# First loads in eight pieces from two queues, a fixed order of the first roundings, eight warm-up products, and pe copied mostly by ScalarE

## The chip, the cores and the metric

The kernel runs on one core of one Trainium2 chip. A core has TensorE (PE, matrix products into PSUM), VectorE (DVE), ScalarE (ACT), GpSimd (POOL) and SyncE (SP, here the engine that issues DMAs). The metric is device microseconds of one execution, lower is better. The kernel before takes 1084.98 us, the median of 3 runs (1084.43 to 1085.68).

## The reference

One layer of a decoder trunk, all in float32, for 1024 tokens of width 1024:

```
h = rms_norm(x, norm_mix_g)
proj = h @ w_in          # q, k, v, z_a, gate, conv B, C, xc, z_c, merge gates g_a, g_c
y_a = (rms_norm(gated linear attention(q, k, v, gate)) * silu(z_a)) @ w_branch_a
y_c = (B * causal_dwconv3(C * xc) * silu(z_c)) @ w_branch_c
x = x + (sigmoid(g_a + b_ga) * y_a + sigmoid(g_c + b_gc) * y_c) @ w_out
gate = sigmoid(rms_norm(x, norm_ple_g) @ w_ple_gate)
x = x + gate * (p @ w_ple_proj)
out = rms_norm(x, norm_final_g)
```

What matters here is `p @ w_ple_proj`, called pe: p is 1024 x 256, the weight 256 x 1024. It depends on nothing but inputs. It is the first real work of the kernel; its result is stored to DRAM and read again near the end.

## The kernel before

Every large product is done in three passes over fp32r operands: each operand is split into a rounded high part and a low part (`hi`, and `lo = src - hi`), and high x high, high x low and low x high are added up in PSUM (`mm3`, line 605). `split` (594) is one rounding copy on ScalarE and one subtraction on VectorE. The large projections use a scheme of seven products of half-size quadrants instead of eight; each quadrant product is a chain of 128x128 by 128x512 products in one PSUM bank.

The program is first written down as a list of operations (`Flow.note`, 270), and a planner puts them in order: `set_dues` (369) counts a due time back from the end, `put_in_order` (416) replays all engines with estimated costs and picks, whenever an engine is free, the ready operation with the earliest due time. TensorE's main products stay in the order in which they were written; products marked as side work (`nc.side`), such as the sums `ms` and the transposes `rt`, are slipped in when ready. `nc.hurry` moves due times earlier. All DMAs are issued by SP, in the order of the plan.

The start runs like this. VectorE clears `zero` (929), and TensorE does nine products of zeros into the banks that pe will use (934), the warm-up. Meanwhile SP loads the first halves of p transposed (`pr_`, in the trace `pTraw`) and of the pe weight (`wr_`, in the trace `wperaw`), each in two pieces of 128 x 512 (kt = 0 and 1), 256 KB a piece (956 to 958). Then come the second half of the weight, x transposed (`hq`) and the rest of p. The pieces are split (1041 to 1045) into `pThi`, `pTlo`, `wpehi`, `wpelo`.

`pe_blocks` (1007) multiplies: a block is 128 tokens by 512 columns, six products (two kt, three passes) in one of six banks. The first four blocks go through kt first: for kt 0 each block's three passes, then the same for kt 1. Each finished block is copied out of PSUM, by VectorE for odd blocks and by ScalarE for even ones (1021), and stored to DRAM (`ped`). There are 16 blocks.

Beside that, `scale_h` (976) computes the norm of x: squares on ScalarE (`sq`), their sums over the partitions on TensorE (`ms`), the power -0.5 on GpSimd (`r_x`), a copy on VectorE that spreads the four columns of `r_x` over 128 columns each (`rb`, 994), four transposes on TensorE (`rt`), and the scaling of `hq` on VectorE. Then `h0hi` and `h0lo` are split off, and the first cells, `ga0p` to `ga3p`, are multiplied with them (`two_products`, 1030). `Cell.product` (751) goes through four kt, three passes each.

The lines that set the first products' order are these:

```
todo = [(b, kt) for kt in range(2) for b in bs] if by_kt else [(b, kt) for b in bs for kt in range(2)]
for b, kt in todo:
    mm3(acc[b - bs[0]], pth[:, kt, rows(b)], ptl[:, kt, rows(b)], wph[:, kt, halves[c]],
        wpl[:, kt, halves[c]], kt == 0, kt == 1)
```

Of the kernel before, what the change touches and what calls it, by code (L numbers as in the profile page):

```python
# [9 lines left out]
F32 = mybir.dt.float32  # L10
# [6 lines left out]
P = 128  # L17
# [239 lines left out]
class Flow:  # L257
# [4 lines left out]

    def __init__(self, tc):
        nc = tc.nc
        self.tc, self.ops, self.side, self.open, self.hurry, self.bundle = tc, [], True, [], 0.0, None
        self.tensor, self.vector, self.scalar = Port(self, PE, nc.tensor), Port(self, DVE, nc.vector), Port(self, ACT, nc.scalar)
        self.gpsimd, self.sync = Port(self, POOL, nc.gpsimd), Port(self, SP, nc.sync)


    def note(self, engine, op, call, args, kw):  # L270
        views = [a for a in args if isinstance(a, View) or hasattr(a, "ap")]
        views += [a for k, a in kw.items() if k not in ("out", "accum_out") and (isinstance(a, View) or hasattr(a, "ap"))]
        outs, ins = ([kw["out"]], views) if "out" in kw else (views[:1], views[1:])
        if kw.get("accum_out") is not None:
            outs.append(kw["accum_out"])
        o = Op()
        o.n, o.engine, o.call, o.args, o.kw = len(self.ops), engine, call, args, kw
        o.side, o.table, o.bytes, o.bufs, o.hurry = self.side, 0, 0, [], self.hurry
        label = lambda v: v.buf.name if isinstance(v, View) else "in"
        o.name = f"{label(outs[0])}<-{','.join(label(v) for v in ins)}"  # L280
        shape = outs[0].shape
        n = 1
        for d in shape[1:]:
            n *= d
        o.lat = 0.15
        if engine == PE:
            o.cost, o.lat = n / 2400 + 0.0134, 0.22
            if op == "transpose" or args[1].dtype == F32:
                o.cost = 0.11
            elif args[1].shape[0] < P:  # L290
                o.cost = 0.42
        elif engine == DVE:
            psum = any(isinstance(v, View) and v.buf.pool.name == "ps" for v in outs + ins)
            o.cost = 0.07 + n * (0.00055 if op in ("tensor_scalar", "tensor_copy") and not psum else 0.00104)
            if op in ("scalar_tensor_tensor", "tensor_scalar"):
                o.cost += 0.06
            if op == "tensor_tensor_scan":
                o.cost = 0.05 + n * 0.0021
        elif engine == ACT:
            o.cost = 0.10 + n * 0.000833 + (0.1 if "accum_out" in kw else 0.0)  # L300
            o.table = TABLE.get(args[2] if len(args) > 2 else None, 0)
        elif engine == POOL:
            o.cost = 0.1 + n * 0.001 if op == "memset" else 0.6
        else:
            o.cost, o.bytes = 0.4, shape[0] * n * 4
            if getattr(ins[0], "apart", None):
                o.cost, o.bytes = 0.6, 1.4 * o.bytes
            o.lat = 2.0 + o.bytes / 250e3
        preds = {}

        def behind(p):
            if p is not None and p != o.n:
                q = self.ops[p]
                lat = q.lat
                if q.engine == engine and engine != SP:
                    lat = 0.0 if engine == PE else 0.08
                preds[p] = max(preds.get(p, 0.0), lat)

        for v in ins:
            if isinstance(v, View):  # L320
                for b in v.blocks():
                    e = v.buf.memory.setdefault(b, [None, []])
                    behind(e[0])
                    e[1].append(o.n)
        for v in outs:
            if isinstance(v, View):
                for b in v.blocks():
                    e = v.buf.memory.setdefault(b, [None, []])
                    for p in [e[0]] + e[1]:
                        behind(p)  # L330
                    e[0], e[1] = o.n, []
                if engine == PE:
                    behind(v.buf.group)
                    v.buf.group = o.n
                for pool in v.buf.pool.instead:
                    for old in pool.buffers:
                        for p in old.users:
                            behind(p)
        for v in outs + ins:
            if isinstance(v, View) and v.buf not in o.bufs:  # L340
                if v.buf.index is None:
                    v.buf.index = len(v.buf.tag.buffers)
                    v.buf.tag.buffers.append(v.buf)
                o.bufs.append(v.buf)
                v.buf.users.append(o.n)
        o.preds, o.succs = preds, []
        for p in preds:
            self.ops[p].succs.append(o.n)
        self.ops.append(o)
        if self.bundle is not None and engine == PE:  # L350
            self.bundle.append(o)
# [163 lines left out]
def kernel(  # L515
# [22 lines left out]
    def f(ap):  # L538
        return ap.bitcast(F32)
# [186 lines left out]
    class Cell:  # L726
# [21 lines left out]
                self.load(k)  # L748
                self.ring[k] = self.steps[k]()

        def product(self, k, acc, start):
            self.prep(k)
            shi, slo = self.ring[k]
            rhi, rlo = self.res[k]
            for kt in range(4):
                nc.side = False
                mm3(acc, shi[:, kt, :], slo[:, kt, :], rhi[:, kt, :], rlo[:, kt, :], start and kt == 0, kt == 3)
                nc.side = True
                if kt % 2 == 1:
                    tick()  # L760
# [165 lines left out]

    hres = [None] * 7
    zero = bp.tile([P, 512], F32R, tag="u2", name="zero", bufs=2)
    nc.vector.memset(f(zero), 0.0)
    ones = sm.tile([P, 1], F32, name="ones")  # L930
    nc.gpsimd.memset(ones, 1.0)
    warm = [psm.tile([P, 512], F32, tag=f"m{i}", name=f"warm{i}") for i in range(6)]
    nc.side = False
    for n in range(9):
        mm(warm[n % 6], zero[:, 0:P], zero, start=True, stop=True)
    nc.side = True

    with phase("prep0") as pool:
# [15 lines left out]

        nc.hurry = 8.0
        for kt in range(2):
            load(pr_[:, kt, halves[0]], pT[:, kt, halves[0]])
            load(wr_[:, kt, halves[0]], wpe[:, kt, halves[0]])
        for kt in range(2):
            load(wr_[:, kt, halves[1]], wpe[:, kt, halves[1]])  # L960
        nc.hurry = 0.0
# [14 lines left out]
        def scale_h(i):  # L976
# [13 lines left out]
            r = sm.tile([P, 4], F32, tag="rx", name=f"r_x{i}", bufs=2)  # L990
            nc.vector.tensor_scalar(r, sums[:, :, 0], EPS, None, op0=ALU.add)
            nc.gpsimd.tensor_tensor(r, r, mhalf[:, 0:1].to_broadcast([P, 4]), op=ALU.pow)
            rb = bp.tile([P, 4, P], F32, tag="u2", name=f"rb{i}", bufs=2)
            nc.vector.tensor_copy(rb, r[:, :, None].to_broadcast([P, 4, P]))
            rt = pso.tile([P, 4, P], F32, tag="o", name=f"rt{i}", bufs=2)
            for s in range(4):
                transpose(rt[:, s, :], rb[:, s, :])
            rt = rt.rearrange("p s t -> p (s t)")
            for n in both:
                for k in range(4):  # L1000
# [6 lines left out]
        def pe_blocks(bs, c, by_kt=False):  # L1007
            acc = []
            for b in bs:
                n = BANKS[at[0]] if at[0] < len(BANKS) else 4 + at[0] % 2  # L1010
                acc.append(psm.tile([P, 512], F32, tag=f"m{n}", name=f"pe{b}_{c}"))
                at[0] += 1
            todo = [(b, kt) for kt in range(2) for b in bs] if by_kt else [(b, kt) for b in bs for kt in range(2)]
            for b, kt in todo:
                nc.side = at[0] > len(BANKS)
                mm3(acc[b - bs[0]], pth[:, kt, rows(b)], ptl[:, kt, rows(b)], wph[:, kt, halves[c]],
                    wpl[:, kt, halves[c]], kt == 0, kt == 1)
                nc.side = True
                if kt == 1:
                    t = bp.tile([P, 512], F32, tag="T", name=f"pe{b}_{c}", bufs=4)  # L1020
                    (nc.vector.tensor_copy if b % 2 else nc.scalar.copy)(t, acc[b - bs[0]])
                    store(ped[b][:, halves[c]], t)

        hb, steps = build_a("h", q)
# [5 lines left out]
        def two_products(cells, banks):  # L1030
            acc = [psm.tile([P, 512], F32, tag=f"m{n}", name=f"{c.name}X") for n, c in zip(banks, cells)]
            for c, X in zip(cells, acc):
                c.product(0, X, True)
                t = ev(f"{c.name}s1")
                nc.scalar.copy(t, X)
                store(s1d[pre.index(c)], t)
            for c, X in zip(cells, acc):
                c.product(3, X, False)
                c.cons(0, 0, X)

        nc.hurry = 8.0
        for kt in range(2):
            split(pth[:, kt, halves[0]], ptl[:, kt, halves[0]], pr_[:, kt, halves[0]])
            split(wph[:, kt, halves[0]], wpl[:, kt, halves[0]], wr_[:, kt, halves[0]])
        nc.hurry = 0.0
        pe_blocks(range(0, 4), 0, True)
        split_half(wph, wpl, wr_, 1)
# [754 lines left out]
```

## Time and profile before

| what | us |
|---|---|
| median of 3 runs | 1084.98 |
| profiled execution, its own time | 1085.03 |
| its span, first to last instruction | 1083.2 |
| TensorE busy | 1071.5 |
| VectorE busy | 870.2 |
| ScalarE busy | 600.3 |
| first warm-up product starts | 1.44 |
| first product of pe starts | 5.55 |
| first product `ga0pX` starts | 30.76 |

A row of the order of time has the start, the time taken, the engine, the line, the operation, what it writes and reads, and in brackets how long the engine had been idle and what released it. Line 503 is the planner's emitter, so all operations of the kernel carry it, and tiles are told apart by name. PEld is TensorE loading weights, SPq is SP issuing a DMA. The chain that ended last has start, time and what worked. A row of stages has the stretch and its length, then busy time of PE, PEld, DVE, ACT and POOL with the number of instructions, the granted clock, the DMA engines' share, and GB/s.

### The profile page before, as it was taken

The numbers are of one execution on the slowest core, as the hardware profiler recorded it, in microseconds if no ns is written. First come the engines' busy times: TensorE is split into PE (matmuls) and PEld (weight loads), VectorE is DVE, ScalarE is ACT, GpSimd is POOL, SyncE is SP. The second block draws the span as 40 slices with busy tenths as digits, with TensorE's granted clock in tenths as the row PEclk, the third lists the DMA queues.
The fourth block names the chain that finished last, engine by engine and source line by source line (L and its number), as shares of the span: only waits on it lengthen the run. The fifth ranks groups of instructions, "written<-read, shape, count | busy, mean of one in ns | idle before, by whom it ended". The sixth has DMA issues, their size and how long they took to land.

```text
span 1083.2 us, 14658 instructions
## 1 busy us (share of the span) xinstructions
PE 1071.5 (99%) x4893; PEld 891.7 (82%) x4893; DVE 870.2 (80%) x1343; ACT 600.3 (55%) x1080; POOL 49.2 (5%) x89
## 2 busy tenths in 40 slices
PE   9999999999999999999999999999999999999996
PEld 7888887888888888888888888888888888888885
DVE  6998667678997977856757788887999888889886
ACT  6778548657453455433333367766756635467554
POOL 0000000000000000000000012110000000012013
PEclk9999999999999999999999999999999999999998
DMA  9943554557776598221222679989586879799954
GB/s 322 321 151 126 185 189 151 165 186 232 219 218 224 193 316 270 74 100 49 70 86 69 235 254 333 332 286 337 195 306 218 282 220 313 238 334 324 318 186 156
DMA packets 144251, 237.85 MB, mean 220 GB/s; under 512 B 11952, under 2 KB 57264, under 8 KB 141232
## 3 DMA queue, kind: packets, MB, share of 16 engines
q1 hardware_dynamic: 144176, 236.93, 64.8%
q8 instruction: 38, 0.62, 0.2%
q14 instruction: 37, 0.30, 0.1%
HBM read 156.14 MB, written 80.74 MB: 219 GB/s over the span
## 4 chain that ended last, share of the span: by engine, by line
PE 97%; DVE 1%; ACT 1%; issue 0%; POOL 0%; DMA 0%; POOLq 0%; DVEq 0%; ACTq 0%
PE vY L503 3%; PE zaY L503 3%; PE pe L503 2%; PE zaV L503 2%; PE vV L503 2%; PE op L503 2%; PE zaX L503 2%; PE vX L503 2%; PE kv L503 1%; PE ga2Y L503 1%; PE ga0Y L503 1%; PE ga1Y L503 1%; PE ga3Y L503 1%; PE gc1Y L503 1%; PE cb3Y L503 1%; PE gc0Y L503 1%
## 5 line engine op out<-in xcount | busy, mean ns | idle before, releaser
L503 ACT ACTIVATE junk<-x 128x512 bf16<-128x512 f32 (+1 forms) x29 | 17.8, 615 | 19.3 <-DVE x L503 14.2
L503 ACT ACT_TABLE_LOAD x18 | 23.1, 1283 | 1.0 <-PEq L1791 0.7
L503 DVE TENSOR_TENSOR wt<-wt 128x512 f32<-128x512 f32 x32 | 21.6, 686 | 0.3
L503 POOL MEMSET t<- 128x2 f32 x8 | 0.8, 99 | 440.4 <-DMA qkd<-kk 241.5
L503 DVE SCALAR_TENSOR_TENSOR u<-t,vec,u 128x1024 f32<-128x1024 f32 x16 | 20.3, 1276 | 0.0
L503 POOL TENSOR_SCALAR rg<-ms 128x1 f32<-128x1 f32 x8 | 6.6, 822 | 261.2 <-ACT junk L503 261.0
L503 ACT ACTIVATE og<-op,or 128x256 f32<-128x256 f32 x32 | 13.3, 468 | 1.7 <-POOL or L503 1.7
L503 ACT CAST S<-S 128x512 fp32r<-128x512 f32 x14 | 8.7, 619 | 9.5 <-PE op L503 9.1
L503 ACT ACTIVATE oq<-oq,vec 128x512 f32<-128x512 f32 x20 | 13.3, 716 | 0.0
L503 PE MATMUL pe<-wpehi,pThi 128*128 128x512 f32 x32 | 13.2, 411 | 0.0
L503 ACT ACTIVATE junk<-op 128x256 bf16<-128x256 f32 x32 | 12.1, 379 | 1.7 <-PE op L503 1.4
L503 PE MATMUL pe<-wpelo,pThi 128*128 128x512 f32 x32 | 12.8, 400 | 0.0
L503 POOL TENSOR_TENSOR or<-or,mhalf 128x2 f32<-128x2 f32 x16 | 12.7, 794 | 1.3
L503 PE MATMUL pe<-wpehi,pTlo 128*128 128x512 f32 x32 | 12.7, 397 | 0.0
L503 PE MATMUL op<-v,aTh 128*128 128x256 f32 x64 | 12.6, 280 | 0.0
L503 DVE TENSOR_TENSOR szl<-og,szl 128x512 f32<-128x512 f32 x16 | 11.0, 685 | 1.7 <-ACT og L503 1.7
L503 DVE SCALAR_TENSOR_TENSOR hq<-hq,vec,rt 128x512 f32<-128x512 f32 x16 | 11.0, 739 | 1.5 <-PE rt L503 1.5
L503 DVE SCALAR_TENSOR_TENSOR S<-S,dds,kv 128x256 f32<-128x256 f32 x24 | 10.4, 473 | 1.8 <-PE kv L503 1.7
L503 DVE STREAM_TRANSPOSE oT<-szl 128x512 f32<-128x512 f32 x16 | 11.3, 704 | 0.2
L503 DVE TENSOR_TENSOR u<-u,s 128x512 f32<-128x512 f32 x16 | 10.9, 687 | 0.3
L503 DVE TENSOR_TENSOR x<-x,pe 128x512 f32<-128x512 f32 (+1 forms) x17 | 10.9, 653 | 0.2
L503 DVE SCALAR_TENSOR_TENSOR x<-x,rf,gfin 128x1024 f32<-128x1024 f32 (+2 forms) x8 | 8.9, 1112 | 2.7 <-POOL rf L503 2.7
(2905 smaller groups left out, 4107.2 us busy)
## 6 DMA issues: line engine op xcount, KB each, us to landing
wtd<-wt SPq DMA_DIRECT2D x44, 256.0 KB, 3.8
wt<-in_wb_dram SPq DMA_DIRECT2D x8, 1024.0 KB, 6.8
v<-vd SPq DMA_DIRECT2D x16, 512.0 KB, 5.8
wgq<-wtd SPq DMA_DIRECT2D x7, 1024.0 KB, 6.6
qk<-qkd SPq DMA_DIRECT2D x12, 512.0 KB, 5.9
vraw<-in_wv_dram SPq DMA_DIRECT2D x20, 256.0 KB, 3.9
zaraw<-in_wv_dram SPq DMA_DIRECT2D x20, 256.0 KB, 4.2
uq<-ud SPq DMA_DIRECT2D x5, 1024.0 KB, 7.7
```

Of the source, the lines that this page charges most:

```text
L503: o.call(*[place(a) for a in o.args], **{k: place(a) for k, a in o.kw.items()})
```

## The change

The planner gets two additions: DMAs issued by an engine other than SP have a cost and a latency of their own, and `nc.hold` adds an order between operations. The memset clears 128 columns only; eight warm-up products read these 128 columns four times. The first loads become eight pieces of 128 x 256 (128 KB): four of p on ScalarE's queue, four of the weight on SP's. The roundings of these pieces have a fixed order on ScalarE and on VectorE, and the rounding of the weight for kt 0 moves to VectorE. In the first four blocks the passes are taken one after the other over all blocks, instead of block by block. In the first cell's first product the four products with `h0lo` come last. `rb` is dropped: the transposes read `r_x` broadcast. Of every four blocks of pe VectorE copies one and ScalarE three.

```diff
+        if op == "dma_start" and engine != SP:
+            o.cost, o.lat = 0.4, 2.3 + shape[0] * n * 4 / 250e3
...
+        if self.hold is not None:
+            preds[self.hold] = max(preds.get(self.hold, 0.0), 0.08)
...
-        def product(self, k, acc, start):
+        def product(self, k, acc, start, late=False):
...
-            for kt in range(4):
+            for n in range(12 if late else 0):
+                kt, w = (n // 2, (shi, slo)[n % 2]) if n < 8 else (n - 8, shi)
+                nc.side = False
+                mm(acc, w[:, kt, :], (rhi if n < 8 else rlo)[:, kt, :], start=n == 0, stop=n == 11)
+                nc.side = True
+            for kt in () if late else range(4):
...
-    nc.vector.memset(f(zero), 0.0)
+    nc.vector.memset(f(zero)[:, 0:P], 0.0)
...
-    for n in range(9):
-        mm(warm[n % 6], zero[:, 0:P], zero, start=True, stop=True)
+    for n in range(8):
+        mm(warm[n % 6].rearrange("p (a b) -> p a b", a=4), zero[:, 0:P], zero[:, None, 0:P].to_broadcast([P, 4, P]), start=True, stop=True)
...
         for kt in range(2):
-            load(pr_[:, kt, halves[0]], pT[:, kt, halves[0]])
-            load(wr_[:, kt, halves[0]], wpe[:, kt, halves[0]])
+            for cs in (slice(0, 256), slice(256, 512)):
+                nc.scalar.dma_start(pr_[:, kt, cs], pT[:, kt, cs])
+                load(wr_[:, kt, cs], wpe[:, kt, cs])
...
-            rb = bp.tile([P, 4, P], F32, tag="u2", name=f"rb{i}", bufs=2)
-            nc.vector.tensor_copy(rb, r[:, :, None].to_broadcast([P, 4, P]))
...
-                transpose(rt[:, s, :], rb[:, s, :])
+                transpose(rt[:, s, :], r[:, s:s + 1].to_broadcast([P, P]))
...
-            todo = [(b, kt) for kt in range(2) for b in bs] if by_kt else [(b, kt) for b in bs for kt in range(2)]
-            for b, kt in todo:
+            some = range(3)
+            if by_kt:
+                todo = [(b, kt, n) for kt in range(2) for n in some for b in bs]
+            else:
+                todo = [(b, kt, n) for b in bs for kt in range(2) for n in some]
+            for b, kt, n in todo:
...
-                mm3(acc[b - bs[0]], pth[:, kt, rows(b)], ptl[:, kt, rows(b)], wph[:, kt, halves[c]],
-                    wpl[:, kt, halves[c]], kt == 0, kt == 1)
+                mm(acc[b - bs[0]], (pth, pth, ptl)[n][:, kt, rows(b)], (wph, wpl, wph)[n][:, kt, halves[c]],
+                   start=kt == n == 0, stop=kt == 1 and n == 2)
...
-                    (nc.vector.tensor_copy if b % 2 else nc.scalar.copy)(t, acc[b - bs[0]])
+                    (nc.vector.tensor_copy if b % 4 == 3 else nc.scalar.copy)(t, acc[b - bs[0]])
...
-                c.product(0, X, True)
+                c.product(0, X, True, c is pre[0])
...
+        left = halves[0]
+        first = {nc.scalar: None, nc.vector: None}
+
+        def then(port, do, *a, **kw):
+            nc.hold = first[port]
+            getattr(port, do)(*a, **kw)
+            nc.hold, first[port] = None, len(nc.ops) - 1
+
+        def low(lo, src, hi):
+            then(nc.vector, "tensor_tensor", lo, src, f(hi), op=ALU.subtract)
+
         nc.hurry = 8.0
-        for kt in range(2):
-            split(pth[:, kt, halves[0]], ptl[:, kt, halves[0]], pr_[:, kt, halves[0]])
-            split(wph[:, kt, halves[0]], wpl[:, kt, halves[0]], wr_[:, kt, halves[0]])
+        for cs in (slice(0, 256), slice(256, 512)):
+            then(nc.scalar, "copy", pth[:, 0, cs], pr_[:, 0, cs])
+        then(nc.vector, "tensor_copy", wph[:, 0, left], wr_[:, 0, left])
+        low(wpl[:, 0, left], wr_[:, 0, left], wph[:, 0, left])
+        low(ptl[:, 0, left], pr_[:, 0, left], pth[:, 0, left])
+        then(nc.scalar, "copy", wph[:, 1, left], wr_[:, 1, left])
+        then(nc.scalar, "copy", pth[:, 1, left], pr_[:, 1, left])
+        low(wpl[:, 1, left], wr_[:, 1, left], wph[:, 1, left])
+        low(ptl[:, 1, left], pr_[:, 1, left], pth[:, 1, left])
```

More of the change, by code (lines that the diff above doesn't have):

```diff
@@ L264, in __init__ @@
         nc = tc.nc
-        self.tc, self.ops, self.side, self.open, self.hurry, self.bundle = tc, [], True, [], 0.0, None
+        self.tc, self.ops, self.side, self.open, self.hurry, self.bundle, self.hold = tc, [], True, [], 0.0, None, None
         self.tensor, self.vector, self.scalar = Port(self, PE, nc.tensor), Port(self, DVE, nc.vector), Port(self, ACT, nc.scalar)
@@ L1012, in pe_blocks @@
                 at[0] += 1
-            todo = [(b, kt) for kt in range(2) for b in bs] if by_kt else [(b, kt) for b in bs for kt in range(2)]
-            for b, kt in todo:
+            some = range(3)
[4 more added lines that the diff above has]
+            for b, kt, n in todo:
                 nc.side = at[0] > len(BANKS)
-                mm3(acc[b - bs[0]], pth[:, kt, rows(b)], ptl[:, kt, rows(b)], wph[:, kt, halves[c]],
-                    wpl[:, kt, halves[c]], kt == 0, kt == 1)
+                mm(acc[b - bs[0]], (pth, pth, ptl)[n][:, kt, rows(b)], (wph, wpl, wph)[n][:, kt, halves[c]],
+                   start=kt == n == 0, stop=kt == 1 and n == 2)
                 nc.side = True
-                if kt == 1:
+                if kt == 1 and n == 2:
                     t = bp.tile([P, 512], F32, tag="T", name=f"pe{b}_{c}", bufs=4)
-                    (nc.vector.tensor_copy if b % 2 else nc.scalar.copy)(t, acc[b - bs[0]])
+                    (nc.vector.tensor_copy if b % 4 == 3 else nc.scalar.copy)(t, acc[b - bs[0]])
                     store(ped[b][:, halves[c]], t)
```

## The prediction

> **What bounds the kernel now.** I read the page first, then the waits of TensorE, then the chain that ended last, and only then the order of time of the first ten microseconds.
>
> ```profile
> span 1083.2 us, 14658 instructions
> ...
> PE 1071.5 (99%) x4893; PEld 891.7 (82%) x4893; DVE 870.2 (80%) x1343; ACT 600.3 (55%) x1080; POOL 49.2 (5%) x89
> ...
> PE warm L503 <- DVE zero L503: 1.4, 1, 1.4
> ...
> 0.90 0.50 DVE zero L503
> 1.44 4.21 PE warm L503 x9
> 5.65 13.95 PE pe L503 x57
> 24.15 6.61 PE pe L503 x29
> 30.76 2.72 PE ga0pX L503 x12
> ```
>
> The third line is the whole list of TensorE's waits: one, at the start. From 1.44 us on TensorE never runs dry, and the chain is TensorE alone for the first 49 us. So nothing in the middle of the kernel can be shortened by lightening another engine; what the change can move is the start: when the first real product begins, and how long TensorE runs at its slow pace. It can also lose, if its new order makes TensorE wait where it does not wait now. The pace in the settled stage is 2.72 / 12 = 0.227 us per product of 128x512.
>
> The start in order of time:
>
> ```profile
> 0.72 1.28 ACT L503 ACT_TABLE_LOAD   x1 [0.72 <-PEq L1791]
> 0.72 0.38 SPq L503 DMA_DIRECT2D wperaw<-in_wpe_dram  x1
> 0.90 0.48 DVE L503 MEMSET zero<- 128x512 f32 x1 [0.90 <-PEq L1791]
> 1.16 0.42 SPq L503 DMA_DIRECT2D pTraw<-in_pT_dram  x1
> 1.63 0.42 SPq L503 DMA_DIRECT2D wperaw<-in_wpe_dram  x1
> 2.10 0.43 SPq L503 DMA_DIRECT2D pTraw<-in_pT_dram  x1
> 3.95 0.62 ACT L503 CAST wpehi<-wperaw 128x512 fp32r<-128x512 f32 x1 [1.95 <-DMA wperaw<-in_wpe_dram]
> 4.88 0.62 ACT L503 CAST pThi<-pTraw 128x512 fp32r<-128x512 f32 x1 [0.31 <-DMA pTraw<-in_pT_dram]
> 5.55 0.29 PEld L503 LDWEIGHTS pe<-wpehi,pThi 128*128 128x128 f32 x1 [0.62 <-ACT pThi L503]
> 5.55 0.79 PE L503 MATMUL pe<-wpehi,pThi 128*128 128x512 f32 x1
> 6.14 0.63 PE L503 MATMUL pe<-wpelo,pThi 128*128 128x512 f32 x1
> 6.57 0.63 PE L503 MATMUL pe<-wpehi,pTlo 128*128 128x512 f32 x1
> 7.00 0.56 PE L503 MATMUL pe<-wpehi,pThi 128*128 128x512 f32 x1
> 7.39 0.40 PE L503 MATMUL pe<-wpelo,pThi 128*128 128x512 f32 x1
> 7.63 0.40 PE L503 MATMUL pe<-wpehi,pTlo 128*128 128x512 f32 x1
> 7.73 0.62 ACT L503 CAST pThi<-pTraw 128x512 fp32r<-128x512 f32 x1 [1.53 <-DMA pTraw<-in_pT_dram]
> ...
> L503 PE MATMUL warm<-zero x9: 632/632/797, 1.4 to 5.0; 128*128 128x512 f32 x9
> ```
>
> The first product starts at 5.55, right behind the rounding of pT (4.88 + 0.62 = 5.50). That rounding waited for its load, issued at 1.16 and usable at 4.88. Products start 0.43 apart up to 7.00 (6.57 - 6.14), and 0.23 to 0.24 apart from 7.39: the pace doubles at about 7.35, which is 5.9 us after the first warm-up product. At the slow pace a microsecond does 0.227 / 0.427 = 0.53 of a microsecond's work. With R the start of real work and F the moment of the full pace, the end therefore moves by 0.53 x (shift of R) + 0.47 x (shift of F), plus any new idle time. All later stages just shift.
>
> **The change part by part.**
>
> *Shorter memset and warm-up.* The memset falls from 512 to 128 columns: of 0.48 us I take 0.20 as an estimate (a quarter of it and some fixed cost; bounds 0.12 and 0.48), so the warm-up begins 0.28 earlier, at 1.16. Eight warm-up products instead of nine end at 1.16 + 0.59 (the first product's spacing, 6.14 - 5.55) + 7 x 0.427 = 4.74. If F follows the start of TensorE's activity, F moves by -0.28 and the end by 0.47 x -0.28 = -0.13. Repeating 128 columns four times as the moving operand I cost at nothing; no row shows that form, the settled 0.227 bounds it below and twice that above, under 8 x 0.2 us, all of it before data are there.
>
> *Loads.* SP issues four loads of 128 KB (0.42 each) where it issued four of 256 KB, so what follows in its queue, the other half of wpe and xT, keeps its time. ScalarE's queue issues four more, about 4 x 0.43 = 1.7 us (SP's rows are the nearest). With the table load of 1.28 that fills ScalarE from 0.72 to about 3.7; it was idle until 3.95, so this is hidden, in either order of the two. Now the bytes:
>
> ```profile
> 0.00:4.00 4.00, 2.56 (x6) 2.10 (x7) 0.48 (x1) 1.33 (x2) 0.75 (x8) 1.00 0.49 154
> 4.00:6.00 2.00, 2.00 (x5) 1.19 (x5) 1.16 (x2) 1.60 (x3) 0.00 (x0) 1.00 0.94 263
> 6.00:8.00 2.00, 2.00 (x7) 1.50 (x7) 0.92 (x2) 0.47 (x2) 0.00 (x0) 1.00 0.95 336
> ```
>
> The last two columns are the DMA engines' share and GB/s: from 4 us on they are full. (The granted clock beside them reads 1.00 even where the products are 0.43 apart; for the clock I go by the spacing.) The first two loads carry 512 KB; the first four pieces of the new order carry the same 512 KB and are issued by the same 1.6 us, if ScalarE issues before its table load. So the last of them lands between 4.0 (when the first load was usable) and 4.85. If the table load goes first, the pT pieces are issued at 2.00 and 2.43 and, with the 3.2 us that the first load took (0.72 to 3.95) less 0.4 for half the bytes, land at 4.8 and 5.2; but the first product needs only the first piece. After landing comes a rounding of 256 columns on ScalarE (about 0.4, estimated from 0.62 for 512) or of 512 on VectorE. So R lies between 4.74 (end of the warm-up) and 5.5. I take 5.15, nearer to the loads' row than to the warm-up's: R moves by -0.40, the end by 0.53 x -0.40 = -0.21.
>
> The Trainium skill, page "DMA: Bandwidth & Descriptors", section "Issuing engines are not separate DMA queues", says that loads issued from several engines share the same 16 DMA engines and save only issue time. By that the second queue alone is worth nothing here and the sum would be -0.13; the full DMA share above agrees with it.
>
> *Fixed order of roundings, products n-major.* The same number of roundings and products. All four high-by-high products come first, so the low parts get 4 to 8 products more time. The second half (kt = 1) needs its rounded pT at the 13th product, about 5.15 + 0.59 + 4 x 0.43 + 7 x 0.227 = 9.05; today's fourth load is usable at 7.73, plus 0.62 = 8.35. Cost nothing; if ScalarE's later issue delays that load by 1.2 us, a gap of up to 0.5. The chain on ScalarE puts pT's second rounding behind that of wpe, which waits for its load; behind both stand the squares and, through them, `ms`. In the first cell's product the four with `h0lo` now come last, which only gives `h0lo` more time.
>
> *`rb` dropped; pe copied by ScalarE.*
>
> ```profile
> L503 DVE COPY rb<-r_x x2: 421/424/426, 23.0 to 47.2; 128x512 f32<-128x512 f32 x2
> 23.48 0.43 PEld L503 LDWEIGHTS rt<-ident,rb 128*128 128x128 f32 x4 [0.21 <-DVE rb L503]
> 21.63 1.34 POOL L503 TENSOR_TENSOR r_x<-r_x,mhalf 128x4 f32<-128x4 f32 x1 [20.31 <-DVE r_x L503]
> L503 ACT COPY pe<-pe x8: 579/587/590, 10.1 to 42.9; 128x512 f32<-128x512 f32 x8
> L503 DVE COPY pe<-pe x8: 680/682/692, 10.8 to 45.0; 128x512 f32<-128x512 f32 x8
> 10.00:20.00 10.00, 10.00 (x49) 8.36 (x48) 7.79 (x10) 8.15 (x12) 0.00 (x0) 1.00 1.05 398
> 30.00:40.00 10.00, 10.00 (x46) 8.29 (x45) 10.00 (x14) 7.69 (x11) 0.00 (x0) 1.00 0.96 316
> 40.00:50.00 10.00, 10.00 (x56) 8.54 (x55) 7.63 (x13) 7.40 (x12) 1.02 (x1) 1.00 0.96 343
> 29.52 1.21 DVE L503 TENSOR_TENSOR h0lo<-hq,h0hi 128x1024 fp32r<-128x1024 f32 x1
> ```
>
> Two copies of 0.42 leave VectorE, and the 0.21 that the weight load waited for `rb` can go. Next late is GpSimd's power, 1.34 us, which the planner books at 0.6: it may place the transposes before the power is done. Bounds -0.21 and +0.3 per use, twice; I take 0. Four pe copies move: VectorE loses 4 x 0.68 = 2.7 us, ScalarE gains 4 x 0.59 = 2.3. VectorE is full from 30 to 40 (10.00 of 10.00), so it gains slack; ScalarE is busy 8.15, 7.69 and 7.40 of 10 in the stages above, so 2.3 us fit over forty. The cover is that the banks are not wanted again at once: copies run up to 45.0, though the pe products end where `ga0pX` begins, at 30.76. If it fails, the roundings queued behind a copy on ScalarE are late and TensorE waits up to 2.3 us. The next deadline, `h0lo` (done at 29.52 + 1.21 = 30.73, its third slice wanted at 30.76 + 7 x 0.227 = 32.35), keeps over 1 us when TensorE comes 0.4 earlier.
>
> **Sum.** -0.13 - 0.21 + 0 = -0.34. The profiled execution took 1085.03 (span 1083.2 and 1.8 around it), 0.05 above the median of 1084.98, so 1084.7 for it and 1084.6 for a median. The bounds are -0.43 - 0.13 - 0.42 = -1.0 and, with R unmoved, +0.5 for kt = 1 and up to +0.6 for the transposes, about +1.0. The runs of before lie between 1084.43 and 1085.68; 0.2% is 2.2 us, about what a measurement of this kernel can tell from no change.
>
> **The rivals.**
>
> *Loads land no earlier.* R stays at 5.55, only the warm-up's -0.13 is left: 1084.85. For it: the full DMA engines; against: less to land and a shorter rounding before the first product.
>
> *The gap restarts the clock (slower).* The warm-up now ends at 4.74 and the first product comes at 5.15 or later; today the ninth product covers nearly all of that. If the half-speed stretch of 5.9 us counts anew from R, F = 5.15 + 5.9 = 11.05, and the end moves by 0.53 x -0.40 + 0.47 x 3.7 = +1.5: 1086.5. It passes 0.2% where 0.53 x (R - 5.55) + 0.47 x (R - 1.45) exceeds 2.2, that is from R = 5.8 on, as when ScalarE's loads come 0.7 late. For it: no row shows the clock rising with a gap before it. Against: the gap is 0.4 us of 5.9. The Trainium skill, "TensorE: Matmul & The Clock Gate", section "What's actually happening", has the clock released by a busy free-running window of 3.4 us; by it a missed window would cost 0.47 x 3.4 = 1.6, an estimate, and F need not follow the warm-up's start at all. The 5.9 us of this trace fit between one and two such windows.
>
> *ScalarE in the way or an order that makes TensorE wait* between 10 and 60 us: up to 2.3 for the copies plus 0.6 for the transposes, 1087 to 1087.5. For it: the planner re-plans all orders; against: no wait of TensorE in the whole trace today, and VectorE is relieved.
>
> *All early*: R at 4.74, F about a microsecond earlier as well: -0.43 - 0.47 - 0.2 = -1.1, 1083.9. F cannot fall far enough to gain 2.2.
>
> **How the numbers follow.** Forecast 0.50, loads no earlier 0.20, clock restart 0.14 (0.06 of it past 0.2%), ScalarE in the way 0.11 (mostly past it), all early 0.05. So slower 0.15; faster by over 0.2% only if several unknowns fall together, 0.05; within 0.2% 0.80. The range reaches from the early case, with half a microsecond of scatter, to the restarted clock with a little of it: 1083.4 to 1086.8.
>
> **What would show it.** Right: the first pe product near 5.15 (4.7 to 5.5), spacing of 0.227 from about 7.1, TensorE without waits after it, product `ga0pX` starting about 0.3 to 0.4 before 30.76, the rest shifted by that. Wrong: a wait of TensorE for pT pieces beyond 5.6, slow spacing past 8, waits for a pe bank, a rounding or `r_x` between 10 and 60 us.

## The result

The changed kernel is slower: 1087.09 us median (1085.62 to 1089.39), against 1084.73 (1084.15 to 1086.56) for the kernel before on the same chips; ratio 1.0022, 95% interval 1.0016 to 1.0028. The profiled execution took 1086.40.

The page, the waits of TensorE and the start of the chain, of the changed kernel:

```profile
span 1084.6 us, 14667 instructions
...
PE 1071.4 (99%) x4892; PEld 891.3 (82%) x4892; DVE 867.4 (80%) x1338; ACT 604.0 (56%) x1086; POOL 49.6 (5%) x89
...
PE pe L507 <- ACT pThi L507: 2.2, 2, 2.0
PE warm L507 <- DVE zero L507: 1.0, 1, 1.0
...
1.15 3.41 DMA pTraw<-in_pT_dram
4.59 5.52 DMA pTraw<-in_pT_dram
10.19 0.63 ACT pThi L507
10.86 10.27 PE pe L507 x44
32.54 2.72 PE ga0pX L507 x12
```

TensorE has as much work as before, but it also waits twice for `pThi`, 2.2 us in all, 2.0 of them at once. The chain no longer begins with TensorE; until 10.86 it runs over two loads of p, one behind the other. `ga0pX` starts 1.78 later than before, and TensorE meets no wait after that: its last product is late by 1.63. The order of time shows the cause:

```profile
0.72 0.89 ACTq L507 DMA_DIRECT2D pTraw<-in_pT_dram  x2
1.04 3.78 PE L507 MATMUL warm<-zero 128*128 128x512 f32 x8 [1.04 <-DVE zero L507]
1.64 1.28 ACT L507 ACT_TABLE_LOAD   x1 [1.64 <-PEq L1820]
3.62 0.41 ACT L507 CAST pThi<-pTraw 128x256 fp32r<-128x256 f32 x1 [0.69 <-DMA pTraw<-in_pT_dram]
3.62 0.35 ACTq L507 DMA_DIRECT2D pTraw<-in_pT_dram  x1
4.59 0.41 ACT L507 CAST pThi<-pTraw 128x256 fp32r<-128x256 f32 x1 [0.57 <-DMA pTraw<-in_pT_dram]
4.59 0.35 ACTq L507 DMA_DIRECT2D pTraw<-in_pT_dram  x1
5.05 1.97 PE L507 MATMUL pe<-wpehi,pThi 128*128 128x512 f32 x4 [0.23 <-ACT pThi L507]
7.78 1.08 PE L507 MATMUL pe<-wpehi,pTlo 128*128 128x512 f32 x4
10.19 0.62 ACT L507 CAST pThi<-pTraw 128x512 fp32r<-128x512 f32 x1 [4.34 <-DMA pTraw<-in_pT_dram]
10.86 1.20 PE L507 MATMUL pe<-wpehi,pThi 128*128 128x512 f32 x4 [2.01 <-ACT pThi L507]
```

ScalarE (the rows ACTq are its DMA issues) issues two p pieces at the start, not four. The third and fourth leave only at 3.62 and 4.59, each right behind a rounding that had waited for the piece two before it. So the second half of p is in place at 10.1 instead of 7.7, and TensorE, through with its first twelve products at 8.7, stands still.

The rule of the prediction fits this execution. The first product came at 5.05 (-0.50), the spacing reached 0.227 near 6.8 (-0.55), so 0.53 x -0.50 + 0.47 x -0.55 = -0.52; the wait adds 10.86 - 8.47 less one product's 0.23 = 2.17; together +1.65, measured +1.63 at the last product (the whole execution is 1.37 longer). The -0.55 is in part luck: with the same start of the warm-up, at 1.04, the full pace came at other moments in other profiled executions (e3 and e8 below). The median lost more, 2.36. The twenty executions fall into two groups by their mean granted clock: eleven at 0.997 with a median of 1086.31, nine at 0.994 to 0.996 with a median of 1088.05. Theory 1 was that the late issue is the loss; theory 2 that a pause of TensorE also drops its clock, which makes the second group; the rivals were contention of the two queues, and the copies moved to ScalarE.

Why the issue is late can be read in the planner. For an operation that uses what an earlier one on the same engine wrote, `behind` books 0.08 us, whatever the earlier one is (cut from `behind`):

```
if q.engine == engine and engine != SP:
    lat = 0.0 if engine == PE else 0.08
```

Until now only SP issued loads. A load issued by ScalarE and rounded by ScalarE falls under this line: the planner believes the piece is there at once, puts the rounding next, and the remaining issues behind it.

### The profile page after: what moved, and what is told of

The parts are those of the page before. It is cut to its first block, busy times and chain, and to the rows that moved or that the text cites. A ratio compares the mean times of both kernels' runs of the same rounds, so it can differ in the third digit from the quotient of the medians.

```text
span 1084.6 us, 14667 instructions
## 1 busy us (share of the span) xinstructions
PE 1071.4 (99%) x4892; PEld 891.3 (82%) x4892; DVE 867.4 (80%) x1338; ACT 604.0 (56%) x1086; POOL 49.6 (5%) x89
## 4 chain that ended last, share of the span: by engine, by line
PE 97%; DMA 1%; ACT 1%; DVE 1%; issue 0%; POOL 0%; POOLq 0%; ACTq 0%; DVEq 0%
PE vY L507 3%; PE zaY L507 3%; PE vX L507 2%; PE zaV L507 2%; PE vV L507 2%; PE op L507 2%; PE pe L507 2%; PE zaX L507 2%; PE kv L507 1%; DMA pTraw<-in_pT_dram 1%; PE ga2Y L507 1%; PE ga0Y L507 1%; PE ga1Y L507 1%; PE ga3Y L507 1%; PE gc1Y L507 1%; PE cb3Y L507 1%
```

## The experiments

Each was timed beside the kernel before on the same chip; its medians there were 1085.01 (e1 to e4), 1085.05 (e5 to e8) and 1085.10 (e9 to e12).

**e1_landing: the planner learns that a load takes time.** Against the changed kernel:

```diff
-                if q.engine == engine and engine != SP:
+                if q.engine == engine and engine != SP and "<-in" not in q.name:
```

> The changed kernel, with one line of the planner altered: an operation on ScalarE that reads what a load issued by ScalarE brings is given the load's landing time, where the changed kernel gives it 0.08 us. All four p pieces then stand ahead of the first rounding on ScalarE. Theory 1 (the third and fourth p piece were issued late, behind roundings that waited): no wait of TensorE for pThi of more than 0.3 us after the first product, the fourth piece usable by 6.5, 1084.0 to 1084.8, so 2 us or more below the changed kernel. Rival (loads on ScalarE's queue are slow in whatever order, since all share the DMA engines): the fourth piece usable after 8, TensorE waits over 1 us, above 1086.

Measured 1086.83 (1084.65 to 1088.71), ratio 1.0016 (1.0008 to 1.0025). The issue row and the waits of TensorE:

```profile
0.72 1.86 ACTq L507 DMA_DIRECT2D pTraw<-in_pT_dram  x4
...
PE ms L507 <- DVE sq L507: 1.1, 1, 1.1
PE warm L507 <- DVE zero L507: 1.0, 1, 1.0
PE pe L507 <- ACT pe L507: 0.9, 1, 0.9
PE pe L507 <- ACT pThi L507: 0.5, 1, 0.5
```

The four issues now stand together, and the wait for `pThi` falls from 2.2 to 0.5; what is left stands before the first product (5.18), and none before the second half, whose rounding starts at 7.42. So the cause of that wait is settled, and the rival of slow queues is out: it had the fourth piece usable after 8. But the time hardly fell and missed the forecast: other waits came up, for a pe copy and for `sq`. The sums `ms` and the last step of the squares that they read, in the kernel before and in e1:

```profile
16.71 1.23 DVE L503 TENSOR_TENSOR sq<-sq 128x1024 f32<-128x1024 f32 x1
19.43 1.84 PE L503 MATMUL ms<-ones,sq 128*128 128x1 f32 x16
...
19.36 1.23 DVE L507 TENSOR_TENSOR sq<-sq 128x1024 f32<-128x1024 f32 x1
20.73 1.92 PE L507 MATMUL ms<-ones,sq 128*128 128x1 f32 x16 [1.11 <-DVE sq L507]
```

TensorE comes to `ms` at about the same time as before, at 19.6 (20.73 less the wait of 1.11) against 19.43, but the squares are done 2.65 later. Their x came later: its first load is issued at 5.08 instead of 3.52. On ScalarE, moreover, the second square (15.59; before, 12.54) now stands behind three pe copies (14.16, 1.55 long). This is the lead to e6.

**e2_one_queue and e3_old_loads: without ScalarE's queue.** Against the changed kernel, e2 and e3:

```diff
-                nc.scalar.dma_start(pr_[:, kt, cs], pT[:, kt, cs])
+                load(pr_[:, kt, cs], pT[:, kt, cs])
```

```diff
-            for cs in (slice(0, 256), slice(256, 512)):
-                nc.scalar.dma_start(pr_[:, kt, cs], pT[:, kt, cs])
-                load(wr_[:, kt, cs], wpe[:, kt, cs])
+            load(pr_[:, kt, halves[0]], pT[:, kt, halves[0]])
+            load(wr_[:, kt, halves[0]], wpe[:, kt, halves[0]])
```

> The changed kernel with all eight pieces issued by SP. Theory 1: no load stands behind a rounding any more, so most of the 2.4 us comes back: 1084.3 to 1085.2, a little above e1_landing, since eight issues of 0.42 on one queue end at about 4.1. Rival (the two queues as such): the same as e1_landing in direction but faster than it. Rival (the cost is in the pe copies, in rb or in the order of the products): stays at 1087.

> The changed kernel with the four 256 KB loads of before from SP; warm-up, fixed roundings, product order, pe copies and dropped rb stay. Theory 1: 1084.3 to 1085.0, first product at 5.0 to 5.5. Rival (pe copies, rb, order of the products): 1086.5 or more.

Measured: e2 1085.45 (1084.87 to 1086.31), ratio 1.0006 (0.9997 to 1.0015); e3 1086.04 (1084.52 to 1086.59), ratio 1.0004 (0.9995 to 1.0013). By the ratios most of the loss is gone, so most of it sat in the loads; both medians still lie above their forecasts. e3 falls in two heaps: five executions between 1084.52 and 1084.88, six between 1086.04 and 1086.59. Its profiled execution is of the upper heap. The row of `ms` and the stages (the granted clock stands ahead of the DMA share):

```profile
19.43 1.92 PE L507 MATMUL ms<-ones,sq 128*128 128x1 f32 x16 [0.33 <-DVE sq L507]
...
18.00:20.00 2.00, 1.67 (x11) 1.17 (x9) 1.95 (x3) 1.76 (x4) 0.00 (x0) 1.00 0.80 285
20.00:22.00 2.00, 2.00 (x15) 1.91 (x15) 1.10 (x3) 1.76 (x3) 0.30 (x1) 0.81 1.02 392
22.00:24.00 2.00, 2.00 (x6) 1.52 (x6) 0.75 (x2) 1.26 (x3) 1.04 (x1) 0.50 0.94 312
24.00:26.00 2.00, 2.00 (x11) 1.65 (x10) 0.19 (x1) 0.00 (x0) 0.00 (x0) 0.83 0.88 272
```

After a wait of 0.3 us and 16 products of one column, TensorE's clock drops to half: the shares below 1.00 make 0.38 + 1.00 + 0.34 = 1.7 us at zero, that is 3.4 us at half. At half pace 3.4 us lose 3.4 x 0.47 = 1.6, which is the distance of the heaps. The profiled execution of e2 (1086.17) shows the same: a wait of 0.20 for `sq`, the sixteen `ms`, and, after about 1.5 us at full pace, shares of 0.69, 0.50 and 0.95 from 22 to 28, again 1.7 us lost. The drop does not follow every such pause: in e1 1.11 us of waiting before the same sixteen left the clock at 1.00. Nor does it explain the whole upper heap of e3, of which three executions have a mean clock of 0.997, like the lower one; e8 shows a second cause that the mean clock does not see.

**e4_loads_only: the kernel before with the loads alone.** Its four loads of the first halves become the eight pieces, with the planner's cost for a load of another engine:

```diff
+        if op == "dma_start" and engine != SP:
+            o.cost, o.lat = 0.4, 2.3 + shape[0] * n * 4 / 250e3
...
-            load(pr_[:, kt, halves[0]], pT[:, kt, halves[0]])
-            load(wr_[:, kt, halves[0]], wpe[:, kt, halves[0]])
+            for cs in (slice(0, 256), slice(256, 512)):
+                nc.scalar.dma_start(pr_[:, kt, cs], pT[:, kt, cs])
+                load(wr_[:, kt, cs], wpe[:, kt, cs])
```

> The kernel before with the eight pieces from two queues and the planner's cost for them, and nothing else of the change. Theory 1: the planner again believes that p is there 0.08 us after its issue and puts the last p piece behind a waiting rounding; TensorE waits 1 to 3 us before its second half: 1086 to 1088. Rival (another part of the change is to blame): 1084.5 to 1085.2.

Measured 1092.96 (1092.01 to 1093.26), ratio 1.0073 (1.0061 to 1.0086). Two rows of its order of time and a wait:

```profile
4.93 0.34 ACTq L505 DMA_DIRECT2D pTraw<-in_pT_dram  x1
10.45 0.62 ACT L505 CAST pThi<-pTraw 128x512 fp32r<-128x512 f32 x1 [3.67 <-DMA pTraw<-in_pT_dram]
...
PE pe L505 <- ACT wpehi L505: 6.4, 1, 6.4
```

Right in direction and short in size: here all roundings of the weight stand behind the late rounding of p on ScalarE as well, so TensorE does not even begin. The loads are to blame. In the whole change, where the first weight is rounded on VectorE in a fixed order, TensorE begins at 5.05 instead of 11.64; that the order is what limits the damage is likely, not shown by itself.

**e5_fill: something to do in the pause.** Against the changed kernel:

```diff
+                if by_kt and (b, kt, n) == (0, 1, 0):
+                    fill = psm.tile([P, 512], F32, tag="m5", name="fill")
+                    for k in range(9):
+                        mm(fill.rearrange("p (a b) -> p a b", a=4), zero[:, 0:P], zero[:, None, 0:P].to_broadcast([P, 4, P]), start=True, stop=True)
```

> The changed kernel with nine products of zeros into an unused bank between its first twelve pe products and the next twelve, that is in the 2.2 us in which TensorE waits for the late p pieces. They add no result. Theory 2 (the wait itself costs about 1.5 us, and in about half of the executions the pause drops TensorE's clock to half for a further 3.4 us, worth 3.4 x (1 - 0.227/0.427) = 1.6): the slow group of executions, 1087.8 to 1089.4, disappears; all within 1085.6 to 1087.0, median 1086.2. Rival (the two groups come from something else): median 1087.1 and a highest time over 1088, or, if the nine products come on top, 1089.

Measured 1089.64 (1087.88 to 1090.66), ratio 1.0043 (1.0029 to 1.0057).

```profile
PE ms L507 <- DVE sq L507: 1.4, 1, 1.4
PE pe L507 <- ACT pe L507: 1.1, 1, 1.1
PE warm L507 <- DVE zero L507: 1.0, 1, 1.0
PE pe L507 <- ACT pThi L507: 0.4, 1, 0.4
```

The wait for `pThi` was filled, and the second half began at 10.66 (10.86 in the changed kernel). But the planner, which knows nothing of the pause, moved other work, and TensorE then waited for a pe copy and for `sq`; three of the five executions have a mean clock of 0.995. The forecast of 1086.2 is missed, and the cause of the two groups stays open here: inconclusive.

**e6_ms_later: `ms` five products later.** Against e3_old_loads:

```diff
-                              + (SIDE if q.engine == PE != e and q.side else 0.0))
+                              + ((1.7 if q.name[:3] in ("ms0", "ms1") else SIDE) if q.engine == PE != e and q.side else 0.0))
```

> e3_old_loads with the 16 one-column products ms put five pe products later in TensorE's order (the planner's delay for side work raised from 0.5 to 1.7 us for these alone). Theory 2: TensorE no longer waits for sq there (0.3 us and an idle stretch of 2.5 us in e3_old_loads), its clock stays up, and the upper group of e3_old_loads, 1086.0 to 1086.6, disappears: median 1084.4 to 1084.8, all below 1085.4. Rival (the 1.7 us of one-column products alone drop the clock): two groups as in e3_old_loads, median near 1086.

Measured 1085.00 (1083.95 to 1086.75), ratio 1.0002 (0.9993 to 1.0010). The wait for `sq` is gone, and no execution has a mean clock under 0.996. But e3 had only one such execution, and by the ratios (1.0002 and 1.0004) the two are not told apart; the median fell by a microsecond with four instead of six executions in the upper heap. The forecast (all below 1085.4) is missed: four of eleven take 1085.4 or more, up to 1086.75 at clock 0.997. So there is a second cause, which the mean clock does not show; e8 finds it.

**e7_copies_rb: the part from `rb` on, alone.** Against the kernel before:

```diff
-            rb = bp.tile([P, 4, P], F32, tag="u2", name=f"rb{i}", bufs=2)
-            nc.vector.tensor_copy(rb, r[:, :, None].to_broadcast([P, 4, P]))
...
-                transpose(rt[:, s, :], rb[:, s, :])
+                transpose(rt[:, s, :], r[:, s:s + 1].to_broadcast([P, P]))
...
-                    (nc.vector.tensor_copy if b % 2 else nc.scalar.copy)(t, acc[b - bs[0]])
+                    (nc.vector.tensor_copy if b % 4 == 3 else nc.scalar.copy)(t, acc[b - bs[0]])
```

> The kernel before with three of four pe copies on ScalarE and without rb, nothing else. Forecast of the prediction: no cost, 1084.7 to 1085.3. Rival (ScalarE gets in the way): a wait of TensorE for a pe bank or a rounding between 10 and 60 us, 1086 or more.

Measured 1084.75 (1084.12 to 1085.52), ratio 0.9997 (0.9988 to 1.0006). The wait view of its start has the one line of before and a new releaser where `rb` stood:

```profile
PEld rt L503 <- POOL r_x L503: 0.2, 1, 0.2
```

No cost, as forecast: with `rb` gone the transposes wait for the power instead, by the same 0.2.

**e8_warm8: the shorter warm-up alone.** Against the kernel before:

```diff
-    nc.vector.memset(f(zero), 0.0)
+    nc.vector.memset(f(zero)[:, 0:P], 0.0)
...
-    for n in range(9):
-        mm(warm[n % 6], zero[:, 0:P], zero, start=True, stop=True)
+    for n in range(8):
+        mm(warm[n % 6].rearrange("p (a b) -> p a b", a=4), zero[:, 0:P], zero[:, None, 0:P].to_broadcast([P, 4, P]), start=True, stop=True)
```

> The kernel before with the memset of 128 columns and eight warm-up products, nothing else. Forecast of the prediction: the warm-up starts 0.3 to 0.4 earlier and the time falls by about 0.13, so 1084.7 to 1085.0. Rival (the pause of 0.7 us between the warm-up's end near 4.8 and the first product at 5.5 delays the full pace): 1086 or more in some executions.

Measured 1086.20 (1084.37 to 1087.00), ratio 1.0007 (0.9999 to 1.0016); eight of eleven executions took 1085.8 or more, three 1084.4 to 1084.9. Products in order of time:

```profile
2.48 2.33 PE L503 MATMUL warm<-zero 128*128 128x512 f32 x5
5.76 0.80 PE L503 MATMUL pe<-wpehi,pThi 128*128 128x512 f32 x1 [0.94 <-ACT pThi L503]
9.77 0.61 PE L503 MATMUL pe<-wpehi,pThi 128*128 128x512 f32 x1
10.20 0.42 PE L503 MATMUL pe<-wpelo,pThi 128*128 128x512 f32 x1
10.46 0.39 PE L503 MATMUL pe<-wpehi,pTlo 128*128 128x512 f32 x1
```

After a pause of 0.94 us the products stay 0.43 apart until 10.2 instead of 7.35. That is 0.47 x 2.9 + 0.53 x 0.21 = 1.5, and its last product is 1.47 late. The ratio's interval still holds no change, but seven of the eleven lie above 1086.02, the highest of the 27 executions of the kernel before on this chip. All eleven have a mean clock of 0.997: the granted clock reads 1.00 in this slow stretch too. So this is the prediction's rival of the restarted clock, by itself, and it leaves the term of -0.13 for the warm-up with the wrong sign. That its price came out is in part luck: it had 5.9 us of slow pace from the first product on, and here they are 4.4, from a first product that comes later. And a pause does not always do it. The profiled execution of e3 paused for 0.83 us at the same place:

```profile
5.41 1.19 PE L507 MATMUL pe<-wpehi,pThi 128*128 128x512 f32 x4 [0.83 <-ACT pThi L507]
```

The next four products begin at 6.44, so these four took 1.03 us, near the full pace, where the first four of e8 took 1.88 (5.76 to 7.64).

**e9 to e12: the pause closed, with and without the late issue.** Theory 3 is that the loss has two parts, the late issue and the pause between warm-up and first product. All have ten warm-up products instead of eight and e6's delay of `ms`:

```diff
-    for n in range(8):
+    for n in range(10):
```

e9 has the planner line of e1, e10 has the loads as the change has them, e11 those of before, e12 all pieces from SP.

> e1_landing (all four p pieces of ScalarE issued ahead of its roundings) with ten warm-up products instead of eight and ms put later as in e6_ms_later. Theory 3 (the change loses in two ways: p's second half is issued late, and a warm-up that ends before the data leaves a pause after which the full pace comes up to 3.4 us later): the pause is closed, no run above 1086, median 1084.2 to 1085.0. Rival (the first pe copies on ScalarE, which stand behind the rounding of the second half of p, hold TensorE for about 1 us as in e1_landing): a wait for ACT pe of 0.5 us or more and a median of 1085.3 to 1086.5.

> The changed kernel with ten warm-up products and ms later, nothing else: it differs from e9_all_early only in that the third and fourth p piece stand behind roundings on ScalarE. Theory 3: TensorE waits about 1.5 to 2.2 us for pThi, so 1.2 to 3.5 us more than e9_all_early: 1086.0 to 1088. Rival (the warm-up alone was the loss): within 0.6 of e9_all_early.

> e6_ms_later (loads of before, all else of the change, ms later) with ten warm-up products instead of eight. Theory 3: the pause of 0.6 us between warm-up and first product is gone, and with it the executions above 1085.4: median 1084.0 to 1084.6, that is 0.4 to 1.0 below the kernel before. Rival (the spread of e6_ms_later has another cause): median 1085.0, up to 1086.7 as there.

> e2_one_queue (eight pieces, all from SP) with ten warm-up products and ms later. Theory 3: 1084.0 to 1084.8, no upper group. Compared with e9_all_early it tells what ScalarE's queue is worth once its loads are issued early: the same within 0.5 if both queues share the DMA engines, over 0.8 better for e9_all_early if issuing from two queues is what counts.

| | median | from, to | ratio to before (95%) |
|---|---|---|---|
| e9 | 1084.82 | 1084.48, 1085.29 | 0.9999 (0.9990 to 1.0008) |
| e10 | 1086.62 | 1085.53, 1088.86 | 1.0019 (1.0010 to 1.0028) |
| e11 | 1084.73 | 1084.37, 1085.74 | 0.9999 (0.9990 to 1.0008) |
| e12 | 1085.19 | 1084.35, 1087.81 | 1.0003 (0.9994 to 1.0012) |

In e9 the four issues stand together, and the second half of p is used at 8.40; TensorE has no wait beyond the warm-up's in the first 60 us. e10 differs from it in the planner line alone, that is in the late issue and what the planner moves with it, and takes 1.80 more. Its product after the pause, and the stages with the granted clock:

```profile
11.02 1.38 PE L507 MATMUL pe<-wpehi,pThi 128*128 128x512 f32 x4 [2.79 <-ACT pThi L507]
...
8.00:10.00 2.00, 0.23 (x2) 0.00 (x0) 0.00 (x0) 0.00 (x0) 0.00 (x0) 1.00 1.00 362
10.00:12.00 2.00, 0.98 (x4) 0.84 (x5) 1.00 (x2) 1.65 (x4) 0.00 (x0) 0.98 0.88 265
12.00:14.00 2.00, 2.00 (x6) 1.52 (x6) 1.50 (x3) 2.00 (x4) 0.00 (x0) 0.50 0.91 283
14.00:16.00 2.00, 2.00 (x8) 1.58 (x7) 1.02 (x2) 1.44 (x3) 0.00 (x0) 0.67 1.03 387
```

Here both costs stand in one execution (1088.71): the wait, and behind it 3.4 us at half clock (0.04 + 1.00 + 0.66 = 1.7 lost). Over an execution 1.7 us lower the mean clock by 0.0016. Four of e10's eleven executions have a mean clock of 0.995 to 0.996 and take 1088.35 to 1088.86; the other seven, at 0.997 and 0.998, take 1085.53 to 1087.23. So theory 2 holds in e10. The changed kernel's own two groups, 1.74 apart, differ in the mean clock by the same; that they have the same cause is likely, but none of its slower executions was profiled.

With ten products, the same memset and the same repeated operand as e8, e9 and e11 have no execution above 1085.8: so it was the pause that delayed e8. e11 and e9 come out alike, so once the order is right the two queues and the eight pieces bring nothing over the old loads. e11 misses its forecast (1084.0 to 1084.6) by a little; its highest time is 1085.74, where e6's with two warm-up products less is 1086.75. e12 misses its forecast too, 1085.19 instead of at most 1084.8, with one execution at 1087.81 and clock 0.995. In its profiled execution TensorE still waits, here for a late landing; the rounding of p's second half in e2 and in e12:

```profile
PE pe L507 <- ACT pThi L507: 1.6, 1, 1.6
...
7.17 0.62 ACT L507 CAST pThi<-pTraw 128x512 fp32r<-128x512 f32 x1 [0.18 <-DMA pTraw<-in_pT_dram]
...
9.38 0.62 ACT L507 CAST pThi<-pTraw 128x512 fp32r<-128x512 f32 x1 [2.41 <-DMA pTraw<-in_pT_dram]
```

SP issues the p pieces at the same times in both, the last two from 3.52 on. So with the same loads the landing varies by 2.2 us between these two executions; why stays open.

e9 and e11 are 0.3 to 0.4 below the kernel before by their medians, inside the interval: no version here is shown to beat it.

## Why the prediction was wrong

- **The loads: the step that failed.** It let ScalarE issue all four p pieces from 0.72 on, "hidden, in either order of the two", the two being issues and table load. A third order was not thought of: issues behind roundings. They left at 3.62 and 4.59. The place to see it was the planner's 0.08 us for a user on the same engine; the prediction took the order of the code for the order of the plan. What it cost: 1.80 between the medians of e9 and e10, about 2.2 by their ratios.
- **SP's queue, "keeps its time".** It did not. The first load of x, before and after:

```profile
3.52 0.43 SPq L503 DMA_DIRECT2D hq<-in_xT_dram  x1
4.95 0.43 SPq L507 DMA_DIRECT2D hq<-in_xT_dram  x1
```

SP had waited for p pieces of ScalarE's queue (the last section shows why). In the changed kernel this is hidden behind TensorE's own wait; in e1 it is part of the 1.1 us before `ms`.
- **The second half (kt = 1)**, "cost nothing", with a gap of up to 0.5 if the issue came 1.2 late. The mechanism was named; the size was off: the fourth issue is 2.5 later than SP's of before (4.59 against 2.10), the gap 2.2.
- **The warm-up, -0.13.** Taken alone it has the wrong sign: +1.1 in the median of e8. The rival of the restarted clock had the mechanism, and the price (+1.5) in part by luck. The premise that the full pace follows the start of the warm-up at a fixed distance, 5.9 us, did not hold: with that start at 1.04, it came at 6.8 in the changed kernel, at 10.2 in e8 and by about 5.4 in e3. In the whole change the first product came at 5.05, not 5.76, so this pause was shorter and in the profiled execution did no harm.
- **A pause later on.** That a pause after the full pace has been reached drops the clock again was not among the rivals. By e10 and the mean clock it makes 9 of 20 executions 1.7 slower; without it the median would be, as an estimate, near the 1086.31 of the other eleven, inside the range.
- **First product at 5.15, second pace near 7.1**: 5.05 and 6.8; the rule for the end held within 0.02 us.
- **Copies and `rb` at nothing**: held (e7). **ScalarE in the way**: not in the changed kernel, since TensorE came late; in e1 and e5, where it came early or the plan was moved, waits for pe copies of 0.9 and 1.1 did appear, and waits of 1.1 and 1.4 for the squares.
- **The second queue.** By the Trainium skill, "DMA: Bandwidth & Descriptors", section "Issuing engines are not separate DMA queues", it saves issue time alone; e11 against e9 agrees, 0.1 apart.

The sum by parts, in medians, each against its own kernel before: e9 -0.28, the late issue +1.80, and +0.84 between e10 and the changed kernel. But a median between two groups jumps with their shares (4 of 11 executions with a dropped clock in e10, 9 of 20 in the changed kernel). By the ratios, 1.0019 and 1.0022, the two are 0.3 apart, inside the intervals, and e9 stands at 0.9999: by them the late issue, with the drops behind its wait, is nearly all of the loss. What the two warm-up products and the place of `ms` add to it in the whole change is not shown.

## What to carry to other kernels

When a DMA moves to an engine that also computes, its place in that engine's order is the change: look for the first instruction that waits ahead of each issue, and for what the planner believes of the load's time. A TensorE pause is dearer than it looks: a pause of 1 to 3 us near the start can cost about 1.5 us more through the clock, in some executions and not in others, so close it with throw-away products before you trim the warm-up. When TensorE is freed upstream, look at what it meets next: in e1 the squares for `ms` were later than before, and the gain turned into a wait downstream.

Where the executions of a kernel fall into two groups, read the list of times and not the median alone.

## What the hardware showed

- A pause can be far shorter than the slow stretch behind it: 0.3 us of waiting and 1.7 us of one-column products (e3), or 2.8 us of waiting (e10), were each followed by about 3.4 us at half clock. In the kernel before the same one-column products run without a wait, and none of its 87 executions beside e1 to e12 has a mean clock under 0.996. The Trainium skill, "TensorE: Matmul & The Clock Gate", section "What's actually happening", gives a free-running window of 3.4 us; the length of these stretches agrees. In the same kernels other executions show no such drop by their mean clock, as a window that runs free would have it.
- One 0.94 us pause between warm-up and first product put the full pace off from 7.35 to 10.2 (e8); one of 0.83 did not (e3).
- The load issued at 4.59 was usable at 10.1, 5.5 us for 128 KB; the first, issued at 0.72, at 3.62. By 4.95 SP had issued the whole weight, a piece of p and the first of x.
- In the changed kernel SP waited as well:

```profile
SPq L507 <- DMA pTraw<-in_pT_dram: 5.1, 4, 3.2
```

The program deals eight completion semaphores in turn to the loads of both queues, so a load of SP waits until the load eight before it has landed, also where that was a late one of ScalarE. SP's fifth load, the ninth of all in the program's order, goes out at 3.61, when the first p piece is there (3.62). TensorE was not held by it in this execution.
